# Delta stage of a two-layer hybrid encoder: the written order binds four engines instead of one

## The chip, the cores and the metric

The kernel runs on one core of one Trainium2 chip. The metric is the device time of one execution in microseconds. The core has five engines that run at the same time, each through its own list of instructions in order: TensorE (matrix products; PE in the profile, and PEld for its weight loads), VectorE (DVE), ScalarE (ACT), GpSimd (POOL) and SyncE (SP), which here only issues transfers. An instruction that needs another engine's result, or a buffer that is still in use, waits on a semaphore, and everything behind it in the same engine's list waits too.

## The reference

Input x is 1 x 2048 x 1024 in float32. Two layers follow one another, then a final RMSNorm. Each layer does this:

```
h = rms_norm(x); proj = h @ w_in                   # 1024 -> 5648 columns
# branch A: gated DeltaNet, 4 heads of 128, both directions
q, k, v = silu(depthwise_conv5(proj[...])); q, k L2-normalised
g = -exp(a_log) * softplus(a + dt_bias); beta = sigmoid(b)
# per chunk: (I + lmat) sol = [v*beta, k*beta*exp(g)]; scan over chunks with a 128x128 state per head
v_new = val - k_cum @ S;  o = q_dec @ S + attn @ v_new;  S = S * decay + k_dec^T @ v_new
o = rms_norm(o_forward + o_backward) * silu(z_a);  y_a = o @ w_dn_out
# branch B: GLU -> depthwise conv 31 -> LayerNorm -> silu, times silu(z_b);  y_b = (...) @ w_cf_out
gate = sigmoid(gate_lg + gate_b)                   # two gates of 1024 columns
x = x + (gate_a * y_a + gate_b * y_b) @ w_out
```

## The kernel before

**Layout.** Channels lie on the 128 partitions and tokens along the free dimension. A dense product takes each operand as a high part and a rest (`split`, lines 161 to 163) and sums three products, so a "dense step" (`dense_steps`, line 174) is three matmuls of 128x128 by 128x512 into one PSUM tile `pd`. Eight such steps make one block of 512 tokens by 128 output columns. A column's weights are loaded and split by `weight` (line 165), which has two buffers each for the high part, the rest and the raw load.

**Order of a layer.** The heads of branch A, the Conformer convolutions and the gate columns of the first half of the tokens come first; then `delta` (line 819), the stage that the change is about; then `merge` (line 1128).

**The Delta stage.** Chunks hold 128 tokens, so there are 16 steps (`NCH`). Step s handles chunk s in the forward direction and chunk 15 - s in the backward one. Its parts are Python generators:

- `fetch` loads a step's keys, queries and values for both directions (`kq`, `kv`) and has GpSimd scale the keys (line 855).
- `prep` makes the inverse of a step's triangular matrix for both directions and four heads. It loads Gram matrices (`dl<-gr`), decay rows (`dm<-gc`, rows spread to all partitions) and the 32x32 inverse blocks (`dh<-inv`); GpSimd adds a mask (line 885), ScalarE takes eight exponentials (line 888), VectorE makes four products of decay and Gram matrix (lines 889 and 890) and two transposes (line 883). Then four stages of small matmuls join 32x32 inverses to 64x64 and then to 128x128, with a ScalarE copy between the first and second (line 911) and between the third and fourth (line 935).
- `lane`, one per direction: in its first stage state times keys and state times queries; VectorE updates the values (line 970) and ScalarE scales the query result (line 961). In its second stage the inverse times the values, copied out by ScalarE (line 977). In its third stage the new state (VectorE, line 987) and the output; from step 8 on the other direction's output of that chunk is loaded back, GpSimd adds the query part (line 998) and VectorE the rest (line 999).
- `finish` normalises two finished chunks (ScalarE squares at line 1012, a reciprocal square root of small VectorE instructions at lines 195 to 201, ScalarE scalings at line 1023); `gate` transposes them on TensorE (line 89) and stores them.
- `pull(n)` takes n dense steps from a filler: the gate columns of the second half of the tokens (`gates(1)`, 256 steps), then an early part of the merge (`early_merge`, 64 steps). The counts are LEAD ahead of the loop, STEP inside a step and TAIL behind it. A filler that yields GAP ends the current step's pulls.

**What sets the order.** A planner orders each engine's instructions by the program's order as a priority and its own estimate of when each is ready, and sets the waits. `set_order` (line 98) chains TensorE's instructions of this stage in the order in which they are written; VectorE, ScalarE, GpSimd and the transfer queues are left to the planner. `prep` runs two steps ahead: steps 0 and 1 are prepared before the loop, and step s carries the four matmul stages of step s + 2. Buffers are rings cut out of larger tiles: four each for `kq` and `kv`, two for decay rows (one step's worth), four and six for Gram matrices, five for outputs, two for gate inputs.

Of the kernel before, what the change touches and what calls it, by code (L numbers as in the profile page):

```python
# [28 lines left out]
LEAD = (20, 8, 8, 6, 4)  # L29
STEP = (5, 4, 4, 3)  # L30
TAIL = (6, 8)
# [4 lines left out]
BIG = -1.0e30  # L36
NOSYNC = mybir.DependencyInfo(mybir.DependencyClass.NoSync, mybir.DependencyReason.DATA)
# [37 lines left out]
class Trunk:  # L75
    def __init__(self, tc, a, depth):
        self.tc, self.nc, self.a, self.depth = tc, tc.nc, a, depth
        self.back = deque()
        self.post = deque()
        self.credit = 0.0  # L80
        self.rate = 0.0
        self.inorder = False
        self.tail = None

    def matmul(self, *args, **kw):
        return self.queue(self.nc.tensor.matmul(*args, **kw))  # L86

    def transpose(self, *args):
        return self.queue(self.nc.tensor.transpose(*args))

    def queue(self, ins):
        if self.inorder:
            if self.tail is not None:
                self.tc.add_manual_dep(ins.ins, self.tail, NOSYNC, reason="TensorE order")
            self.tail = ins.ins.name
        return ins

    def set_order(self, on):
        self.inorder, self.tail = on, None
# [74 lines left out]
    def dense_steps(self, ps, w, xs, kk):  # L174
        mm = self.matmul
# [625 lines left out]
    def gates(self, half):  # L801
        nc = self.nc
        for j in range(16):
            w = self.weight(self.a["w_in"][self.l, 28 + j], KD)
# [14 lines left out]
    def delta(self):  # L819
# [26 lines left out]
        def fetch(step):  # L846
            out = []
            for d in range(2):
# [5 lines left out]
                k2 = col(self.kf, d, c)  # L854
                nc.gpsimd.tensor_tensor(out=kv[:, 0], in0=kv[:, 0], in1=k2[:, :, None].to_broadcast([P, 4, P]),
                                        op=ALU.mult)
                out.append((c, kq, kv))
            return out

        blk = lambda b: slice(32 * b, 32 * b + 32)  # L860
        lo, up = slice(0, 64), slice(64, 128)
        pairs = ((0, 1), (2, 3))

        def prep(step):
            ins, ks = [], []
# [3 lines left out]
            quads = range(4)  # L869
            for d in range(2):  # L870
                c = step if d == 0 else NCH - 1 - step
                g, k = hv(rgq()), hv(rgk())
                self.load(g, self.g_d[c][:, :, 1, :])
                self.load(k, self.g_d[c][:, :, 0, :])
                gb = hv(rgb())
                v32 = (dt if d == 0 else pt)[:, d]
                with nc.allow_non_contiguous_dma(reason="rows to all partitions and inverse blocks"):
                    r0 = d * 64 + c * 4
                    self.load(gb, self.gc_d[r0:r0 + 4][None].to_broadcast([P, 4, P]))
                    r4 = 64 * d + 4 * c  # L880
                    self.load(v32, self.inv_d[:, r4:r4 + 4, :].rearrange("h b (i j) -> (b i) h j", j=32))
                o32 = (pt if d == 0 else dt)[:, d]
                v_.transpose(o32.rearrange("p h c -> p (h c)"), v32.rearrange("p h c -> p (h c)"))
# [5 lines left out]
                v_.tensor_tensor(out=k, in0=k, in1=gb, op=ALU.mult)  # L889
                v_.tensor_tensor(out=g, in0=g, in1=gb, op=ALU.mult)  # L890
                ins.append(g)
                ks.append(k)
            yield
            wt = rwt().rearrange("p (m c) -> p m c", c=P)
# [7 lines left out]
            mm = self.matmul  # L902
# [46 lines left out]
        def lane(step, d, g, wt, c, kq, kv):  # L949
            mm = self.matmul  # L950
# [3 lines left out]

            def query():
                pq = hv(self.pz())
                for hd in range(H):
                    mm(pq[:, hd, :], kq[:, hd, 1, :], s[:, hd, :], start=True, stop=True)
                o1 = ro1()
                for hd in range(H):  # L960
                    nc.scalar.activation(hv(o1)[:, hd, :], pq[:, hd, :], AF.Copy, scale=eg[:, hd:hd + 1])  # L961
                return o1
# [345 lines left out]
```

## Time and profile before

| what | value |
|---|---|
| time, median of 3 runs | 3299.22 us (3292.3 to 3299.87) |
| the profiled execution's own time | 3296.47 us |
| its span, first to last instruction | 3294.7 us |
| TensorE / its weight loads / VectorE busy | 95% / 83% / 72% |
| ScalarE / GpSimd busy | 42% / 9% |
| mean granted TensorE clock | 0.981 |
| bytes moved by DMA | 501.69 MB, mean 152 GB/s |
| Delta stage, first product to last transpose | about 900 to 1329 us and 2507 to 2942 us |

Busy time of TensorE includes modelled ends of its pipelined matmuls. The granted clock is 1.00 at full rate; a stretch that shows less had a part at half rate. "Idle before" counts the time in which an engine had nothing running ahead of an instruction, with the one that ended the wait behind the arrow. Line 86 is a helper that records every matmul, so TensorE's work is told apart by tiles: `pd` is dense work, `pz` is the Delta stage's; `dl`, `dm` and `dh` are the tiles that the rings are cut from.

### The profile page before, as it was taken

The numbers are of one execution on the slowest core, as the hardware profiler recorded it, in microseconds if no ns is written. First come the engines' busy times: TensorE is split into PE (matmuls) and PEld (weight loads), VectorE is DVE, ScalarE is ACT, GpSimd is POOL, SyncE is SP. The second block draws the span as 40 slices with busy tenths as digits, with TensorE's granted clock in tenths as the row PEclk, the third lists the DMA queues.
The fourth block names the chain that finished last, engine by engine and source line by source line (L and its number), as shares of the span: only waits on it lengthen the run. The fifth ranks groups of instructions, "written<-read, shape, count | busy, mean of one in ns | idle before, by whom it ended". The sixth has DMA issues, their size and how long they took to land. (4 is left out here: it accounts for less than half of the span.)

```text
span 3294.7 us, 51078 instructions
## 1 busy us (share of the span) xinstructions
PE 3127.2 (95%) x19110; PEld 2727.5 (83%) x19110; DVE 2360.0 (72%) x4401; ACT 1391.8 (42%) x3104; POOL 303.4 (9%) x297
## 2 busy tenths in 40 slices
PE   6999999999999988999999999999999998998998
PEld 5888888888788878787888888888887887887786
DVE  7689989896555566745676989898864556567655
ACT  5625252523443456523344333343234444565332
POOL 3000000000121221000000000000002112200000
PEclk9999999999999999999999999999999999899999
DMA  4223131334676776654423232323457767756634
GB/s 140 89 94 109 65 109 65 110 115 161 225 248 219 245 219 196 193 184 129 140 62 94 76 101 87 97 80 97 154 194 235 238 220 216 231 180 199 202 124 150
DMA packets 425880, 501.69 MB, mean 152 GB/s; under 512 B 95584, under 2 KB 260064, under 8 KB 425632
## 3 DMA queue, kind: packets, MB, share of 16 engines
q1 hardware_dynamic: 352304, 387.53, 38.3%
q10 hardware_dynamic: 65264, 81.14, 7.1%
q0 software_dynamic: 8064, 29.76, 2.4%
q8 instruction: 150, 2.46, 0.3%
q14 instruction: 98, 0.80, 0.1%
HBM read 342.74 MB, written 155.58 MB: 151 GB/s over the span
## 5 line engine op out<-in xcount | busy, mean ns | idle before, releaser
L86 PE MATMUL pd<-hhi,whi 128*128 128x512 f32 x2816 | 1100.1, 391 | 0.0
L86 PE MATMUL pd<-hhi,wlo 128*128 128x512 f32 x2816 | 1078.2, 383 | 2.9 <-DVE wlo L163 2.9
L86 PE MATMUL pd<-hlo,whi 128*128 128x512 f32 x2816 | 1078.7, 383 | 0.0
L740 DVE SCALAR_TENSOR_TENSOR cacc<-gp,vec,cacc 128x1009 f32<-128x1009 f32 (+1 forms) x480 | 614.0, 1279 | 37.7 <-ACT cacc L738 34.6
L86 PEld LDWEIGHTS pd<-hhi,wlo 128*128 128x128 f32 x2816 | 538.2, 191 | 81.9 <-DVE wlo L163 4.5
L86 PEld LDWEIGHTS pd<-hhi,whi 128*128 128x128 f32 x2816 | 538.8, 191 | 81.0 <-issue 1.4
L86 PEld LDWEIGHTS pd<-hlo,whi 128*128 128x128 f32 x2816 | 539.1, 191 | 74.2 <-issue 1.9
L162 ACT ACTIVATE whi<-wraw 128x512 fp32r<-128x512 f32 x400 | 243.0, 624 | 437.1 <-PE pd L86 340.4
L163 DVE TENSOR_TENSOR wlo<-wraw,whi 128x512 fp32r<-128x512 f32 x400 | 272.7, 695 | 118.0 <-ACT whi L162 117.6
L565 DVE SCALAR_TENSOR_TENSOR acc<-cin,vec,acc 128x1022 f32<-128x1022 f32 (+1 forms) x192 | 246.4, 1298 | 15.0 <-ACT acc L563 13.9
L86 PE MATMUL pd<-yhi,wlo 128*128 128x512 f32 x512 | 195.3, 381 | 6.7 <-DVE wlo L163 6.5
L86 PE MATMUL pd<-yhi,whi 128*128 128x512 f32 x512 | 194.9, 381 | 2.1 <-ACT whi L162 2.0
L86 PE MATMUL pd<-ylo,whi 128*128 128x512 f32 x512 | 194.3, 379 | 1.7 <-DVE ylo L163 1.7
L888 ACT ACTIVATE dm<-dm,ngc 128x128 f32<-128x128 f32 x256 | 89.3, 403 | 216.8 <-POOL dm L885 214.7
L86 PEld LDWEIGHTS pz<-dh,dl 32*32 32x32 f32 (+2 forms) x2496 | 144.8, 148 | 26.7 <-DVE dl L889 10.0
L86 PE MATMUL pz<-dh,dl 32*32 32x32 f32 (+2 forms) x2496 | 151.6, 235 | 15.8 <-DVE dl L889 9.6
L86 PE MATMUL pd<-uop,whi 128*128 128x512 f32 x512 | 157.9, 390 | 6.5 <-ACT whi L162 6.5
L86 PE MATMUL pd<-gop,whi 128*128 128x512 f32 x512 | 153.8, 382 | 4.9 <-DVE gt L1164 3.4
L889 DVE TENSOR_TENSOR dl<-dl,dm 128x512 f32<-128x512 f32 x64 | 46.1, 721 | 153.7 <-ACT dm L888 113.1
L86 PEld LDWEIGHTS pz<-dm,dl 128*128 128x128 f32 x992 | 119.0, 198 | 17.0 <-issue 15.6
L86 PE MATMUL pz<-dm,dl 128*128 128x128 f32 x992 | 121.2, 282 | 10.0 <-ACT dm L977 9.7
L815 ACT ACTIVATE go<-pd,vec 128x512 f32<-128x512 f32 x128 | 87.7, 685 | 83.1 <-PE pd L86 73.0
(272 smaller groups left out, 4242.8 us busy)
## 6 DMA issues: line engine op xcount, KB each, us to landing
wraw<-w_in SPq DMA_DIRECT2D x240, 256.0 KB, 2.9
gt<-go ACTq DMA_DIRECT2D x128, 256.0 KB, 2.8
dl<-gr SPq DMA_DIRECT2D x128, 256.0 KB, 5.5
dl<-kq SPq DMA_DIRECT2D x64, 512.0 KB, 6.4
dl<-kv SPq DMA_DIRECT2D x64, 512.0 KB, 5.3
gt<-gt SPq DMA_DIRECT2D x64, 512.0 KB, 5.0
wraw<-w_out SPq DMA_DIRECT2D x96, 256.0 KB, 3.1
kq<-acc SPq DMA_DIRECT2D x16, 1024.0 KB, 5.4
```

The costliest lines, as they stand in the source:

```text
L86: return self.queue(self.nc.tensor.matmul(*args, **kw))
L162: self.nc.scalar.activation(hi, src, AF.Copy)
L163: self.nc.vector.tensor_tensor(out=lo, in0=src, in1=hi.bitcast(F32), op=ALU.subtract)
L565: self.nc.vector.scalar_tensor_tensor(out=out, in0=t[:, k:k + n], scalar=wc(k), in1=out, op0=ALU.mult, op1=ALU.add)
L740: self.nc.vector.scalar_tensor_tensor(out=acc, in0=t[:, k:k + n], scalar=wc(k), in1=acc, op0=ALU.mult, op1=ALU.add)
L815: nc.scalar.activation(cut(o), sort(ps), AF.Identity, bias=self.vec[:, V_GB + j:V_GB + j + 1])
L888: nc.scalar.activation(gb[:, hd, :], gb[:, hd, :], AF.Exp, bias=ng[:, hd:hd + 1])
L889: v_.tensor_tensor(out=k, in0=k, in1=gb, op=ALU.mult)
```

## The change

The manual chaining of TensorE's instructions goes. After the whole stage has been written, `bind` walks through its instructions and chains each to the one before it on the same engine, for TensorE, ScalarE, VectorE and GpSimd. Transfers on SP stay with the planner; those issued from ScalarE's queue are part of its order.

The text is then laid out as one pipeline. `prep` is cut into more stages: loads; mask and exponentials; transposes, copies and the four products; then the four matmul stages. The loads of step s + 3, the exponentials and products of step s + 2 and the matmul stages of step s + 1 stand in step s, so the inverse is one step ahead instead of two, and only step 0 is prepared whole before the loop. The scaling of the next step's keys is a function of its own (`decay_keys`). In `lane` the loading of the other direction's output and GpSimd's addition move from the third stage to the first. `finish` takes over `gate` and is cut into four stages that are spread over the following step. Weights in `gates` and `early_merge` are asked for one column ahead; the early merge's operands are loaded first and split one by one, with a GAP after each. LEAD, STEP and TAIL get other counts, and a GAP ends only the pull that meets it.

```
-LEAD = (20, 8, 8, 6, 4)
-STEP = (5, 4, 4, 3)
-TAIL = (6, 8)
+LEAD = (16, 6, 8, 6, 4)
+STEP = (5, 4, 4, 4)
+TAIL = (3, 3, 3)
+BOUND = (mybir.EngineType.PE, mybir.EngineType.Activation, mybir.EngineType.DVE, mybir.EngineType.Pool)
...
+    def bind(self, start):
+        last = {}
+        for ins in self.nc.cur_bb.bb.instructions[start:]:
+            if ins.engine in BOUND:
+                if ins.engine in last:
+                    self.tc.add_manual_dep(ins, last[ins.engine], NOSYNC, reason="written order")
+                last[ins.engine] = ins.name
...
     def gates(self, half):
+        ahead = self.weight(self.a["w_in"][self.l, 28], KD)
         for j in range(16):
-            w = self.weight(self.a["w_in"][self.l, 28 + j], KD)
+            w = ahead
+            if j < 15:
+                ahead = self.weight(self.a["w_in"][self.l, 29 + j], KD)
...
         def lane(step, d, g, wt, c, kq, kv):
+            o1 = old = None
+            if step >= NCH // 2:
+                old = ro()
+                self.load(old, od)
             if step:
...
+                if old is not None:
+                    nc.gpsimd.tensor_tensor(out=old, in0=old, in1=o1, op=ALU.add)
             yield
...
+        start = self.mark()
+        nil = iter(())
+        preps = [prep(i) for i in range(NCH)] + [nil, nil, nil]
+        go = lambda i: next(preps[i], None)
+        go(0)
         ins = fetch(0)
+        go(0)
+        go(0)
+        go(1)
         pull(LEAD[0])
+        go(1)
+        go(1)
+        for d in range(2):
+            decay_keys(ins[d], d)
+        for n in LEAD[1:4]:
+            go(0)
             pull(n)
+        go(2)
+        ready = go(0)
+        pull(LEAD[4])
+        last = finish([])
         for step in range(NCH):
             nxt = fetch(step + 1) if step + 1 < NCH else None
+            gs, wt = ready
             lanes = [lane(step, d, gs[d], wt, *ins[d]) for d in range(2)]
+            for x in lanes:
+                next(x)
+            go(step + 1)
+            if nxt:
+                for d in range(2):
+                    decay_keys(nxt[d], d)
+            go(step + 2)
+            next(last)
+            pull(STEP[0])
+            for x in lanes:
+                next(x)
+            next(last)
+            go(step + 2)
+            go(step + 1)
+            pull(STEP[1])
             for x in lanes:
                 next(x, None)
+            go(step + 1)
+            go(step + 3)
+            new = finish(list(done))
             done.clear()
+            next(new)
+            pull(STEP[2])
+            next(last)
+            ready = go(step + 1)
+            last = new
+            pull(STEP[3])
             ins = nxt
+        for n in TAIL:
             pull(n)
+            next(last)
         for _ in fill:
             pass
+        self.bind(start)
...
     def early_merge(self):
+        self.u0, load, split = self.operand_parts(self.u_d, 0, "uop")
         for k in range(4):
+            load(k)
         yield GAP
+        ahead = self.weight(self.a["w_cf"][self.l, 0], 4)
+        for k in range(4):
+            split(k)
+            yield GAP
```

## Prediction before the run

> **What bounds the kernel now.** I read the page first, then a table by stretches of the Delta stage, then who TensorE waits for in it, then the order of time on the engines inside one step.
>
> ```profile
> span 3294.7 us, 51078 instructions
> PE 3127.2 (95%) x19110; PEld 2727.5 (83%) x19110; DVE 2360.0 (72%) x4401; ACT 1391.8 (42%) x3104; POOL 303.4 (9%) x297
> ```
>
> TensorE is busy for 95% of the span, so what any reordering can win is the other 5% and what a slowed clock costs. The second view is the table of busy times by stretches (start:end, length, then busy us and count of PE, PEld, DVE, ACT, POOL, then the granted clock, DMA share, GB/s). Per layer the rows are: lead-in and step 0; step 1; steps 2 to 7; steps 8 to 12; steps 13 and 14; and, for the first layer only, what follows.
>
> ```profile
> 900.20:948.50 48.30, 42.69 (x511) 36.12 (x511) 23.64 (x53) 23.07 (x58) 12.28 (x10) 0.93 0.89 282
> 948.50:973.70 25.20, 22.39 (x242) 20.12 (x241) 14.13 (x39) 13.15 (x31) 4.62 (x4) 1.00 0.71 228
> 973.70:1118.60 144.90, 138.25 (x1441) 122.58 (x1440) 81.13 (x228) 57.14 (x168) 27.74 (x24) 0.98 0.70 225
> 1118.60:1256.50 137.90, 120.92 (x1234) 107.81 (x1234) 87.93 (x256) 71.70 (x247) 36.77 (x31) 0.96 0.73 227
> 1256.50:1300.60 44.10, 38.33 (x344) 35.06 (x343) 29.73 (x85) 28.26 (x84) 8.07 (x6) 0.88 0.68 221
> 1300.60:1329.10 28.50, 28.50 (x172) 25.94 (x171) 13.47 (x45) 18.53 (x55) 2.54 (x2) 1.00 0.54 151
> 2507.10:2559.00 51.90, 45.06 (x512) 38.06 (x512) 24.28 (x53) 22.77 (x58) 11.83 (x11) 0.90 0.85 273
> 2559.00:2583.20 24.20, 22.31 (x242) 20.09 (x241) 13.89 (x38) 13.15 (x31) 4.61 (x4) 1.00 0.69 217
> 2583.20:2726.80 143.60, 136.19 (x1442) 120.38 (x1441) 82.08 (x228) 57.14 (x168) 27.74 (x24) 1.00 0.71 227
> 2726.80:2869.60 142.80, 127.94 (x1234) 113.17 (x1233) 88.55 (x256) 71.80 (x247) 37.19 (x31) 0.90 0.71 218
> 2869.60:2913.40 43.80, 36.60 (x343) 33.81 (x342) 29.66 (x85) 28.06 (x83) 7.91 (x6) 0.92 0.67 219
> ```
>
> To know what of a step is waste I need its TensorE work at full clock. The pieces come from the timeline (start, us, engine, line, tiles, count, and the wait before it in brackets), the filler's price from the chain of waits (start, us, what).
>
> ```profile
> 2473.53 20.52 PE pd L86 x95
> ...
> 2618.05 0.62 PE L86 MATMUL pz<-dh,dh 32*32 32x32 f32 x48 [0.90 <-ACT dh L911]
> 2621.62 3.81 PE L86 MATMUL pz<-dm,dl 128*128 128x128 f32 x32 [0.17 <-ACT dm L977]
> ...
> 2777.35 1.04 PE L89 MATMUL pz<-con,dm 128*128 128x128 f32 x8
> 2778.32 0.68 PE L86 MATMUL pz<-dl,dh 64*64 64x64 f32 x16
> ...
> 2780.98 4.12 PE L86 MATMUL pz<-dh,dl 128*128 128x128 f32 x64
> 2788.04 1.05 DVE L199 TENSOR_TENSOR rst<-orr,rsv 128x8 f32<-128x8 f32 x1
> 2789.27 0.15 DVE L200 TENSOR_TENSOR rst<-rst,orr 128x8 f32<-128x8 f32 x1
> 2789.74 2.05 PE L86 MATMUL pz<-dl,dl 128*128 128x128 f32 x16 [1.21 <-DVE dl L970]
> 2791.00 2.45 ACT L1023 ACTIVATE dm<-dm,orr 128x128 f32<-128x128 f32 x8 [1.93 <-DVE orr L1020]
> ```
>
> State products with the inverse's first product 4.12, inverse's second 0.62, two products of 0.68 (one row stands for both), the triangular product 2.05, state and output products 3.81: 11.96 us. One filler step is three matmuls of 20.52/95 = 0.216, so 0.648; sixteen make 10.4. A step is worth 22.3 us, and 23.4 with the eight transposes (1.04) that appear from step 9.
>
> Length minus work, first layer and second. Lead-in with step 0 holds 42 fillers (27.2), three inverses of 2.4 (0.62 + 0.68 + 0.68, and 0.4 left of the 4.12 when thirty-two products go at the 3.81 row's rate), 2.05 and 3.81: 40.3, so 8.0 and 11.6 are lost. Step 1: 2.9 and 1.9. Steps 2 to 7 (133.8): 11.1 and 9.8. Steps 8 to 12 (115.9): 22.0 and 26.9. Steps 13 and 14 (two fillers, then sixteen without an inverse: 14.3 + 21.0): 8.8 and 8.5. What follows is full: nothing. In all 111.5 us; everything the change can win lies there. That includes the half-rate clock (11 us of it in steps 8 to 12 of layer one, by 2 x 0.04 x 137.9).
>
> Who ends the waits, second layer, first half and second half (us in total, times, longest):
>
> ```profile
> PE pz L86 <- ACT dh L911: 8.3, 7, 2.5
> PE pz L86 <- DVE dl L889: 4.4, 2, 3.6
> ...
> PE pz L86 <- ACT dh L911: 8.7, 5, 2.4
> PE pz L86 <- ACT dm L977: 3.9, 2, 2.5
> PE pz L86 <- DVE dl L970: 3.6, 3, 1.9
> ```
>
> L911 is the small ScalarE copy between the inverse's first two products. The timeline shows why it is late: eight scalings L1023 (2.45 us), themselves late behind a reciprocal square root on VectorE, stand ahead of it on ScalarE. That root's small steps are also mixed among the L970 updates for which the triangular product waited 1.21.
>
> **The change, part by part.** It removes no arithmetic. It fixes ScalarE's, VectorE's and GpSimd's order to the text's, so each wait now also holds whatever is written behind it. Prices, from the groups by line of steps 8 to 12, second layer (busy us, mean ns, idle before):
>
> ```profile
> L888 ACT ACTIVATE dm<-dm,ngc 128x128 f32<-128x128 f32 x40 | 13.9, 395 | 25.9 <-POOL dm L885 25.7
> L885 POOL TENSOR_TENSOR dm<-dm,con 128x512 f32<-128x512 f32 x10 | 13.2, 1318 | 21.1 <-DMA dm<-gc 18.7 <-ACT dm L961 2.4
> L998 POOL TENSOR_TENSOR dm<-dm,dm 128x512 f32<-128x512 f32 x10 | 12.7, 1274 | 20.2 <-ACT dm L961 19.5 <-DMA dm<-o 0.7
> L855 POOL TENSOR_TENSOR dl<-dl,kf 128x512 f32<-128x512 f32 x11 | 11.4, 1040 | 65.2 <-DMA dl<-kv 47.3 <-PE pd L86 9.0 <-PE pz L86 8.9
> L977 ACT ACTIVATE dm<-pz 128x512 f32<-128x512 f32 x10 | 5.5, 591 | 0.3
> L815 ACT ACTIVATE go<-pd,vec 128x512 f32<-128x512 f32 x10 | 6.8, 683 | 0.6 <-DMA dl<-gr 0.5
> L889 DVE TENSOR_TENSOR dl<-dl,dm 128x512 f32<-128x512 f32 x10 | 6.9, 689 | 23.2 <-ACT dm L888 19.5 <-POOL dm L998 3.7
> ```
>
> First-half step, from the start of the state products: these and the first inverse product end at 4.1, five fillers at 7.4, the triangular product at 9.4, the second inverse product at 10.1, four fillers at 12.7; then the next product needs L977's copy. ScalarE's written order ahead of that copy is: scaled queries (to about 5), L911, eight exponentials (3.2). These wait for two GpSimd masks behind two decays, 2 x 1.32 + 2 x 1.04 = 4.7 us. The loads are asked for a step earlier, in the same SP queue, so the masks end near 5 and the copy at about 10.7, against 12.7: covered, with 2 us over. L911 is now written ahead of every scaling and its use four fillers later. I keep 0.4 a step for what I have missed (between 0 and today's 1.7): steps 2 to 7 win 20.9 - 4.8 = 16, step 1 wins 4.8 - 1.0 = 3.8.
>
> Second-half step: the two L998 additions now stand ahead of the decays on GpSimd, because they are written into the lane's first stage. They need the scaled queries (about 3 and 5) and the loads of the old output. The chain is then 6.3 after two additions, 8.4 after the decays, 11.0 after the masks, 12.6 after the last exponentials, 13.2 after the copy, or 13.9 when one L815 falls between: 0.5 to 1.2 later than the 12.7 at which TensorE wants it. VectorE's products (four of 0.69) wait for the same exponentials, and behind them stand the inverse's copies and the state update: another 0.8 by the same addition. With 0.7 for the clock, 2.5 a step. Bounds: 0, and today's 4.9. Ten steps win 48.9 - 25 = 24.
>
> The clock, by the row: steps 8 to 12 of layer two show 0.90 though no wait listed there is longer than 2.5 us, and I charge for it. The Trainium skill, "TensorE: Matmul & The Clock Gate", section "What's actually happening", says that half rate follows an idle window of about 3.4 us. This trace disagrees, since shorter waits sufficed. By the rule my 0.7 a step would go, and the sum would be 7 us better.
>
> Lead-in: it prepares one inverse ahead of the loop instead of two, with 40 fillers instead of 46. ScalarE's written order puts the second inverse's exponentials ahead of the first's L911. Their row load shares buffers with the first's products: loads 5.2 (median below), four products 2.8, another load 5.2, mask 2.6, the last four exponentials 1.6, copy 0.3: 17.7, against a cover of 16 + 6 fillers and one product (14.7). So 3.0 remain, and about 2 for the clock: 5 a layer, between 0 and today's 8.0 and 11.6. Gain 19.6 - 10 = 9.6.
>
> Filler change-over: LEAD 46 and 16 a step leave 2 of the 256 gate fillers for step 13 today. LEAD 40 and 17 a step run out in step 12 after 12; the next five pulls each meet a gap (the operand loads, then four splits one by one), so steps 12 and 13 have 5 and 13 fewer where today one step has 14 fewer. The splits also stand in ScalarE's and VectorE's order now. I charge 10 a layer against 8.8 and 8.5: minus 3, between plus 6 and minus 12.
>
> Parts at nothing: weights asked for one column earlier and the load order (no wait of TensorE above names them); the tail (its row is full, PE 28.50 of 28.50, and 17 filler steps instead of 18 follow); step 0's stores moving to SP. Without that cover the tail's ScalarE and VectorE work would cost about 5 us a layer, from 2.45 and its neighbours.
>
> Sum: 16 + 3.8 + 24 + 9.6 - 3 = 50. The profiled execution's 3296.5 less 50 is 3246; the median of the runs (3299.2) stands 2.7 above that execution, so I forecast 3249 us.
>
> **The rivals.** (1) *Slower: the old output arrives late.* Place: steps 8 to 13, GpSimd's first addition. Issues on SP and the landing times of these tiles:
>
> ```profile
> 2781.69 0.60 SPq L150 DMA_DIRECT2D dm<-o  x1
> ...
> 2815.01 0.42 SPq L150 DMA_DIRECT2D dm<-o  x1
> DMA to landing us min/median/max: 2.8/5.2/7.9
> ```
>
> The steps begin at 2780.98 and 2809.53, so these went out 0.7 and 5.5 in; with 5.2 they land 6 to 11 in, where 5 is wanted. Today only an addition late in the step waits; in the written order decays, masks, exponentials and the state's copy all stand behind it. Each us costs TensorE one: 12 for twelve steps. Landing 4 us later than I allow eats the gain; 11 to 13 in gives 3249 + 12 x 7 = 3333. Against it: the load is written ahead of the state products, earlier than now.
>
> (2) *VectorE blocked by GpSimd.* One root step took 1.05 us (L199) while a mask ran, its neighbour 0.15. In the written order all fourteen follow the L970 updates, just when GpSimd works without a pause; VectorE then reaches the products 2 us later, and steps 8 to 12 keep today's 4.9: 3249 + 24 = 3273, up to 3285 if the first half keeps half of its own. The Trainium skill, "SBUF — State Buffer", section "Who interferes with whom", has this as a rule: a VectorE instruction with two SBUF inputs is blocked whole by a GpSimd one that reads SBUF; the L199 row agrees.
>
> (3) *Nearly all waits go.* If loads land early and the splits hide, only the change-over and the lead-in keep about 20: 3299 - 91 = 3208. The idle 58% of ScalarE speaks for it.
>
> (4) *No change:* the planner's order was as good on average, and each wait removed reappears elsewhere: 3299.
>
> **How the numbers follow.** Forecast (3235 to 3270) 0.42, rival 2 0.13, rival 3 0.17, no change 0.10, slower 0.18. About 0.3%, 10 us, is what a measurement of this kernel can tell from none. Faster 0.42 + 0.13 + 0.17 = 0.72; same 0.10; slower 0.18. The range runs from just below rival 3 to just past no change, 3203 to 3312, leaving out most of rival 1.
>
> **What would show it.** Right: steps 2 to 7 near 23 us each (17 fillers), TensorE's waits on L911 and L970 gone, in steps 8 to 12 a wait of 1 to 2 us on the copy of the triangular product, and 4 to 8 us lost in step 13. Wrong: GpSimd idle for the old output ahead of its additions (rival 1), VectorE's root steps near 1 us and waits on the state update (rival 2), or new waits on L911 in the lead-in beyond 5 us.

## The result, and the profile after

The changed kernel takes 3320.5 us (median of 4 runs, 3318.6 to 3326.9) against 3299.6 us for the kernel before (median of 4 in the same comparison). The ratio is 1.0069, with a 95% interval of 1.0047 to 1.0092: 21 us slower. The forecast was 3249 us with a range that ended at 3312. The sign was wrong, and the time lies outside of the range.

The head of the page of the changed kernel:

```profile
span 3316.8 us, 50988 instructions
...
PE 3129.0 (94%) x19110; PEld 2725.5 (82%) x19110; DVE 2397.4 (72%) x4401; ACT 1400.9 (42%) x3104; POOL 299.4 (9%) x297
```

The arithmetic is the same on every engine, and the span is 22 us longer. The table by stretches (columns as in the prediction) tells where. The rows are steps 13 and 14 of the first layer, then of the second layer the lead-in with step 0, steps 1 to 7, 8 to 12, 13 and 14, and the stretch from step 15 to the first product of the merge's output gate.

```profile
1250.57:1316.40 65.83, 47.66 (x468) 42.86 (x465) 38.88 (x102) 34.90 (x109) 11.50 (x10) 0.82 0.53 169
2510.58:2571.31 60.73, 50.89 (x445) 42.82 (x444) 26.83 (x54) 22.84 (x51) 13.89 (x12) 0.92 0.87 278
2571.31:2739.70 168.39, 163.31 (x1702) 146.01 (x1701) 98.88 (x266) 73.45 (x200) 31.09 (x27) 0.99 0.73 232
2739.70:2870.82 131.12, 120.35 (x1234) 106.87 (x1232) 97.43 (x250) 71.86 (x242) 34.97 (x30) 0.97 0.73 227
2870.82:2935.36 64.54, 45.55 (x466) 40.84 (x464) 37.91 (x102) 34.00 (x107) 11.52 (x10) 0.84 0.53 169
2935.36:2974.87 39.51, 38.52 (x211) 33.39 (x209) 21.34 (x57) 25.20 (x65) 2.56 (x2) 1.00 0.58 172
```

Steps 13 and 14 stand out: 64.5 us with TensorE busy for 45.6, at a granted clock of 0.84. To compare kernels whose steps hold different numbers of fillers, I take from each stretch's length the work of its own matmuls at full clock, as the prediction did, but counted one by one: 0.216 us for a filler matmul, 0.117 for a 128x128 one (3.81 us for 32, less the modelled end of the last), 0.042, 0.013 and 0.13 for the two small shapes and a transpose. For the changed kernel that makes 47.3, 159.3, 114.7, 39.2 and 37.4 us a layer. The row of steps 13 and 14 above then loses 64.54 - 39.2 = 25.3. Counted like this the kernel before loses 116.6 us in both layers (the prediction, by pieces of a step, had 111.5).

| kernel (loss in us, both layers) | time, us | ratio to before, 95% | lead-in, step 0 | 1-7 | 8-12 | 13-14 | rest | sum |
|---|---|---|---|---|---|---|---|---|
| before | 3299.6 | 1 | 20.3 | 28.3 | 51.2 | 18.2 | -1.4 | 116.6 |
| forecast | 3249 | | 10 | 5.8 | 25 | 20 | 0 | 61 |
| changed kernel | 3320.5 | 1.0047 to 1.0092 | 27.2 | 18.6 | 33.5 | 52.1 | 3.3 | 134.7 |
| e1_uop | 3302.6 | 0.9992 to 1.0018 | 26.8 | 22.1 | 32.0 | 33.4 | 3.7 | 118.0 |
| e2_weights | 3283.4 | 0.9936 to 0.9965 | 21.2 | 8.8 | 21.1 | 50.3 | -0.4 | 101.0 |
| e3_both | 3260.6 | 0.9850 to 0.9911 | 19.7 | 9.0 | 17.5 | 34.9 | -0.4 | 80.7 |
| e4_pe_only | 3254.4 | 0.9832 to 0.9899 | 12.7 | 31.5 | 5.2 | 15.0 | -0.2 | 64.2 |
| e5_no_gpsimd | 3227.6 | 0.9764 to 0.9804 | 20.2 | 5.3 | -0.4 | 24.4 | -0.1 | 49.4 |
| e6_first_half | 3244.4 | 0.9800 to 0.9852 | 15.1 | 13.2 | 15.6 | 18.2 | -0.4 | 61.7 |
| e7_add_late | 3234.2 | 0.9784 to 0.9824 | 21.1 | 7.0 | -0.4 | 24.5 | -0.4 | 51.8 |
| e8_old_text | 3525.3 | 1.0665 to 1.0710 | 58.2 | 81.1 | 91.9 | 58.3 | 54.7 | 344.2 |
| e9_add_only | 3273.2 | 0.9894 to 0.9932 | 27.4 | 23.4 | 1.9 | 38.2 | 3.1 | 94.0 |
| e10_lead | 3217.5 | 0.9732 to 0.9768 | 2.6 | 15.7 | -0.4 | 22.3 | -0.4 | 39.8 |
| e11_step16 | 3225.4 | 0.9750 to 0.9784 | 20.8 | 1.6 | -0.2 | 16.5 | -0.8 | 37.9 |
| e12_all | 3205.0 | 0.9691 to 0.9728 | 2.7 | 3.9 | -0.2 | 16.1 | -0.9 | 21.6 |

The sums carry the times: time less sum lies between 3178 and 3190 in every row. That spread, some 12 us, comes from one execution to the next and from outside of the stage (its first load starts between 883.8 and 891.4 us in the builds, with nothing changed ahead of it), so the columns tell smaller differences apart than the times do.

Against the kernel before, steps 1 to 12 gained 27 us; the lead-in lost 7, steps 13 and 14 lost 34, and the rest lost 5. Who ends TensorE's waits in the changed kernel: the lead-in of the second layer, steps 8 to 12 of the second layer, steps 13 and 14 of the first; and whom GpSimd waits for, in two rows for steps 8 to 12 and in the last for steps 13 and 14 of the second layer (us in total, times, longest).

```profile
PE pd L175 <- DVE wlo L157: 7.9, 1, 7.9
...
PE pz L992 <- ACT dm L985: 5.0, 3, 2.9
PE pz L1001 <- DVE dh L931: 3.4, 3, 1.7
...
PE pz L992 <- ACT dm L985: 7.9, 1, 7.9
PE pz L983 <- ACT dm L977: 5.2, 1, 5.2
...
POOL dm L979 <- ACT dm L977: 77.9, 6, 20.1
POOL dm L979 <- DMA dm<-o: 22.6, 1, 22.6
...
POOL dm L979 <- DMA dm<-o: 3.3, 1, 3.3
```

Four things are to be read here. The longest wait in the lead-in names a *weight split* (L157, the rest of a split operand), which no line of the prediction had on its list. Line 985, the copy of the triangular product, waits for 8 us in step 13. Line 931 is one of the inverse's copies on VectorE. And GpSimd's addition of the old output (L979) waits in steps 8 to 12 six times for the scaled queries of its own step and once for the load of the old output; in step 13 that load ends a wait again.

**The lead-in.** The timeline of the second layer's (start, us, engine, line, tiles, count, wait before):

```profile
2511.60 2.63 DVE L902 COPY dl<-dh 32x256 f32<-32x256 f32 x4 [10.38 <-POOL dl L839]
...
2516.59 0.69 DVE L906 TENSOR_TENSOR dl<-dl,dm 128x512 f32<-128x512 f32 x1 [1.63 <-DMA dl<-gr]
2517.20 1.29 DVE L908 TENSOR_TENSOR dl<-dl,dm 128x512 f32<-128x512 f32 x2
2518.40 1.29 DVE L157 TENSOR_TENSOR wlo<-wraw,whi 128x512 fp32r<-128x512 f32 x2
...
2519.14 0.79 PE L175 MATMUL pd<-hhi,wlo 128*128 128x512 f32 x1 [7.94 <-DVE wlo L157]
```

VectorE's order has the first inverse's copies and products ahead of the filler's split, as they are written there. The copies wait for GpSimd to clear their buffer, a product waits for its Gram matrix, and the split stands behind both, with the fillers that were to cover just these waits.

**Step 9, second layer.** Same columns, engines mixed by time:

```profile
2768.18 1.05 PE L968 MATMUL pz<-dh,dl 128*128 128x128 f32 x8
2770.32 1.12 ACT L977 ACTIVATE dm<-pz,eg 128x128 f32<-128x128 f32 x4
2771.52 1.27 POOL L979 TENSOR_TENSOR dm<-dm,dm 128x512 f32<-128x512 f32 x1 [19.25 <-ACT dm L977]
2773.17 1.28 POOL L979 TENSOR_TENSOR dm<-dm,dm 128x512 f32<-128x512 f32 x1 [0.39 <-ACT dm L977]
2773.32 1.15 DVE L1032 TENSOR_TENSOR oss<-oss,cq 128x8 f32<-128x8 f32 x1
2774.41 2.04 POOL L857 TENSOR_TENSOR dl<-dl,kf 128x512 f32<-128x512 f32 x2
2776.41 2.50 POOL L889 TENSOR_TENSOR dm<-dm,con 128x512 f32<-128x512 f32 x2
2777.71 2.50 ACT L892 ACTIVATE dm<-dm,ngc 128x128 f32<-128x128 f32 x8 [4.45 <-POOL dm L889]
2777.74 1.20 DVE L194 TENSOR_TENSOR rst<-rst,orr 128x8 f32<-128x8 f32 x1
2780.12 1.05 ACT L985 ACTIVATE dm<-pz 128x512 f32<-128x512 f32 x2
2780.84 1.13 PE L992 MATMUL pz<-dm,dl 128*128 128x128 f32 x8
2785.03 0.29 DVE L931 COPY dh<-pz 32x128 f32<-32x128 f32 x1
2785.46 1.13 PE L1001 MATMUL pz<-dm,dl 128*128 128x128 f32 x8 [1.70 <-DVE dh L931]
```

GpSimd stood idle for 19 us ahead of L979 with decays (L857) and masks (L889) behind it, since the scaled queries that the addition needs don't exist before this step's own products. Only then did the masks run, and the exponentials (L892) and the copy (L985) after them.

**Step 13, first layer**, the same view:

```profile
1249.24 4.52 SPq L144 DMA_DIRECT2D uop<-u  x4
1255.96 2.48 SPq L144 DMA_DIRECT2D dm<-o  x1
1257.18 1.06 ACT L156 ACTIVATE uop<-uop 128x1024 fp32r<-128x1024 f32 x1 [3.26 <-DMA uop<-u]
1258.14 2.16 ACT L977 ACTIVATE dm<-pz,eg 128x128 f32<-128x128 f32 x8
1259.35 1.28 POOL L979 TENSOR_TENSOR dm<-dm,dm 128x512 f32<-128x512 f32 x1 [20.92 <-ACT dm L977]
1263.79 1.26 POOL L979 TENSOR_TENSOR dm<-dm,dm 128x512 f32<-128x512 f32 x1 [3.16 <-PE pz L983]
1268.30 2.50 ACT L892 ACTIVATE dm<-dm,ngc 128x128 f32<-128x128 f32 x8 [7.82 <-POOL dm L889]
1270.70 1.04 ACT L156 ACTIVATE uop<-uop 128x1024 fp32r<-128x1024 f32 x1
1271.64 1.05 ACT L985 ACTIVATE dm<-pz 128x512 f32<-128x512 f32 x2
1272.36 2.04 PE L992 MATMUL pz<-dm,dl 128*128 128x128 f32 x8 [7.94 <-ACT dm L985]
```

ScalarE's order has a split of the merge's operand (L156) ahead of the query scaling. It waits for its load; the scaling comes at 1258.14, 7.6 us into the step; the first addition waits for the scaling, which ends at 1260.30. The second starts at 1263.79, 3.2 us after the first has ended. The row puts that wait down to a product (L983), but in the second layer the same wait, 3.3 us, is put down to the load of the old output, and that load goes out late here too: its issue stands at 1255.96, 5.4 us into the step, behind the operand's four loads in SP's list. The masks wait for the additions, the exponentials for the masks and the copy for the exponentials, with a second operand split between. This step has hardly a filler to cover it.

### The profile page after: what moved, and what is told of

It is laid out like the page before. It is cut to its first block, busy times and chain, and to the rows that moved or that the text cites. A ratio compares the mean times of both kernels' runs of the same rounds, so it can differ in the third digit from the quotient of the medians.

```text
span 3316.8 us, 50988 instructions
## 1 busy us (share of the span) xinstructions
PE 3129.0 (94%) x19110; PEld 2725.5 (82%) x19110; DVE 2397.4 (72%) x4401; ACT 1400.9 (42%) x3104; POOL 299.4 (9%) x297
## 5 line engine op out<-in xcount | busy, mean ns | idle before, releaser
L175 PE MATMUL pd<-hhi,wlo 128*128 128x512 f32 x2816 | 1075.1, 382 | 18.6 <-DVE wlo L157 18.6
L156 ACT ACTIVATE whi<-wraw 128x512 fp32r<-128x512 f32 x400 | 242.5, 623 | 483.2 <-PE pd L174 312.2
L157 DVE TENSOR_TENSOR wlo<-wraw,whi 128x512 fp32r<-128x512 f32 x400 | 276.4, 706 | 217.4 <-ACT whi L156 216.7
L535 ACT ACTIVATE cin<-pd 128x512 f32<-128x512 f32 x96 | 57.0, 594 | 156.8 <-PE pd L175 156.6
L1192 ACT ACTIVATE gt<-gt 128x1024 f32<-128x1024 f32 x64 | 67.6, 1057 | 114.9 <-DMA gt<-gt 100.8
L175 PEld LDWEIGHTS pd<-yhi,wlo 128*128 128x128 f32 x512 | 96.7, 189 | 22.0 <-DVE wlo L157 8.5
L973 DVE SCALAR_TENSOR_TENSOR dl<-pz,neg,dl 128x128 f32<-128x128 f32 x240 | 66.8, 345 | 66.2 <-PE pz L968 65.9
L892 ACT ACTIVATE dm<-dm,ngc 128x128 f32<-128x128 f32 x256 | 80.2, 391 | 81.1 <-POOL dm L889 80.8
L173 PEld LDWEIGHTS pd<-yhi,whi 128*128 128x128 f32 x512 | 96.8, 189 | 20.3 <-ACT whi L156 7.1
L173 PE MATMUL pd<-uop,whi 128*128 128x512 f32 x256 | 100.2, 391 | 11.9 <-ACT uop L156 6.4
L746 ACT ACTIVATE ao<-pd 128x512 f32<-128x512 f32 x64 | 38.3, 598 | 170.0 <-PE pd L175 169.9
```

The lines of the kernel that those rows point to most:

```text
L156: self.nc.scalar.activation(hi, src, AF.Copy)
L157: self.nc.vector.tensor_tensor(out=lo, in0=src, in1=hi.bitcast(F32), op=ALU.subtract)
L173: mm(ps, whi[:, k, :], xhi, start=k == 0, stop=False)
L175: mm(ps, wlo[:, k, :], xhi, start=False, stop=k == kk - 1)
L535: nc.scalar.activation(cut(t[:, o + b * NB:o + (b + 1) * NB]), sort(ps), AF.Copy)
L892: nc.scalar.activation(gb[:, hd, :], gb[:, hd, :], AF.Exp, bias=ng[:, hd:hd + 1])
```

## The experiments

The first theory from these rows: filler work in the order of other engines costs time, the operand splits in step 13 and the weight splits in the lead-in. Two edits tell the two apart, with this addition to `split` (the weights' splits in one, the operand's in the other):

```
+        if loose: self.loose |= {a.ins.name, b.ins.name}
...
-            if ins.engine in BOUND:
+            if ins.engine in BOUND and ins.name not in self.loose:
```

**e1_uop**: the operand's splits are left to the planner.

> The changed kernel with one thing taken out of the written order: the four splits of the early merge's operands (ScalarE and VectorE, eight instructions a layer) are left to the planner. Theory 1, the splits' place in the order: in step 13 ScalarE's scaling of the query result stands behind the first split, which waits for its operand to land, and the state's copy behind the second. Steps 13 and 14 lose 28.6 and 27.3 us now (length less work); that falls by about 12 a layer, so about 3296 us. Rival, late transfers: the other direction's output still lands some 13 us into step 13, because its load stands behind the operand loads in SP's queue; GpSimd's chain stays and the gain is under 5 us a layer, so 3310 or more.

Measured 3302.6 us, 18 less than the changed kernel. It comes from where it should: steps 13 and 14 fall from 52.1 to 33.4, the other columns stay within 4. The time lies between the two expectations, and the rival holds in part: in step 13 GpSimd still waits 3.9 us in the first layer and 3.6 in the second for the load of the old output, and TensorE's wait on the copy is 9.5 and 9.1 us.

**e2_weights**: the weights' splits are left to the planner.

> The changed kernel with the splits of the fillers' weights left to the planner, everything else bound. Theory 1: the wait of 8.2 and 7.9 us that TensorE has in the lead-in on VectorE's part of a weight split goes, because that split no longer stands behind the inverse's products, which wait for their Gram matrices. With the half-rate clock behind it about 9 us a layer, so about 3302 us. Rival: the lead-in is set by its transfers (their engines are nearly full there), the same wait turns up at the inverse's first product, and the gain is under 3 us a layer, so 3314 or more.

Measured 3283.4 us, 37 less, twice what the lead-in's wait alone could give. The lead-in gives 6; steps 1 to 7 give 10 and steps 8 to 12 another 12. The weight splits cost in steps 1 to 12 too, not in the lead-in alone: the waits of TensorE on the inverse's copy L931 in steps 1 to 7, 4.4 us in the first layer and 3.3 in the second, are no longer listed.

**e3_both**: both kinds are left to the planner.

> Both kinds of split left to the planner. Theory 1: the two gains add, about 42 us, so about 3278 us, faster than the kernel before. Rival, late transfers: 3300 to 3312 us.

Measured 3260.6 us, 60 less and 17 below the expectation: 18 and 37 add, and 5 us are over. With that the change is faster than the kernel before by 1.2%.

**e4_pe_only**: the new text, with TensorE alone bound as in the kernel before.

```
-BOUND = (mybir.EngineType.PE, mybir.EngineType.Activation, mybir.EngineType.DVE, mybir.EngineType.Pool)
+BOUND = (mybir.EngineType.PE,)
```

> The changed kernel's text with TensorE alone bound, as in the kernel before. If the binding of the three other engines is what costs, the time falls to the kernel before's or below, 3280 to 3300 us. If the new text costs (fillers used up earlier, five gaps instead of one, one inverse ahead), it stays at 3312 us or more, with the same 13 fewer fillers in step 13.

Measured 3254.4 us, 26 below the range for the case that the binding costs. So the new text by itself wins 45 us, and binding the three other engines takes 66 away. The columns show both sides of binding: against this kernel, e3_both wins 22 in steps 1 to 7 and loses 12 in steps 8 to 12, 20 in steps 13 and 14 and 7 in the lead-in. Something else than the splits is badly placed from step 8 on. What begins there is the old output.

**e5_no_gpsimd**: as e3_both, and GpSimd is left to the planner.

```
-BOUND = (mybir.EngineType.PE, mybir.EngineType.Activation, mybir.EngineType.DVE, mybir.EngineType.Pool)
+BOUND = (mybir.EngineType.PE, mybir.EngineType.Activation, mybir.EngineType.DVE)
```

> Edit: as the version in which the splits of both operands are left to the planner (3260.6 us), and GpSimd's instructions too; ScalarE, VectorE and TensorE stay in the written order. Theory (what binding still costs there, about 10 us a layer in steps 13 and 14 and 5 in steps 8 to 12 against TensorE alone bound, comes from GpSimd's chain: additions of the old output written ahead of decays and masks): GpSimd can then run a mask ahead of an addition whose load is late, and steps 8 to 14 get back 10 to 15 us a layer, 3230 to 3245. Rival (the cost is ScalarE's and VectorE's own order: copies and squares standing ahead of the copy that TensorE wants): GpSimd's freedom changes nothing, 3255 to 3265, with the wait on the copy of the triangular product in step 13 still near 11 us.

Measured 3227.6 us, a little better than the theory's range. Steps 8 to 12 lose nothing any more (-0.4), steps 13 and 14 lose 24 instead of 35. In steps 8 to 12 GpSimd's order was the rest of the cost; ScalarE's and VectorE's own orders were not. In steps 13 and 14 this version still loses 9 us more than the one with TensorE alone bound (24.4 against 15.0), and which of the two orders costs them no run here tells.

**e7_add_late**: as e3_both, all four bound, with one line of the text moved: GpSimd's addition goes back to the lane's third stage, where the kernel before had it.

```
                 for hd in range(H):
                     nc.scalar.activation(hv(o1)[:, hd, :], pq[:, hd, :], AF.Copy, scale=eg[:, hd:hd + 1])
-                if old is not None:
-                    nc.gpsimd.tensor_tensor(out=old, in0=old, in1=o1, op=ALU.add)
...
             if old is not None:
+                nc.gpsimd.tensor_tensor(out=old, in0=old, in1=o1, op=ALU.add)
                 v_.tensor_tensor(out=old, in0=po, in1=old, op=ALU.add)
```

> Edit: the splits left to the planner, all four engines bound, and GpSimd's addition of the old output moved back from the lane's first stage to its third, behind the triangular product, where the text before had it. Theory (the addition that waits for the old output's load delays decays, masks, exponentials and the state's copy behind it): steps 8 to 12 and 13 to 14 lose less, 3240 to 3252, and the wait on the copy in step 13 falls from 11 us to under 5. Rival (the copy is late for another reason, such as the squares and output products on ScalarE and VectorE): 3257 to 3270, the later addition only delaying the outputs.

Measured 3234.2 us, 6 below the theory's range and far from the rival's. Steps 8 to 12 again lose nothing, and steps 13 and 14 lose 24.5, as with GpSimd free. TensorE's wait on the copy in step 13 falls from 11.1 and 11.3 us (e3_both, by layer) to 2.7 and 2.6. So it is this one instruction's place, and not that GpSimd is bound.

**e6_first_half**: as e3_both, with ScalarE, VectorE and GpSimd bound in steps 0 to 7 only.

```
+        for n, ins in enumerate(self.nc.cur_bb.bb.instructions[start:], start):
+            if ins.engine != mybir.EngineType.PE and not a <= n < b:
+                continue
```

> Edit: the splits left to the planner, and ScalarE, VectorE and GpSimd held to the written order only in steps 0 to 7; in the lead-in and from step 8 on TensorE alone is held. Theory (binding helps where nothing late stands in the order, that is in steps 1 to 7, and costs where the old output and the change-over come in): lost time a layer about 7 in the lead-in, 4.5 in steps 1 to 7, 3 in steps 8 to 12, 7.5 in steps 13 and 14, together 22 against 40 (both sorts of splits loose) and 32 (TensorE alone held): 3225 to 3240. Rival (the gain of steps 1 to 7 is only moved: what is not waited for there is waited for later, since the gate fillers run out at the same place): no better than TensorE alone held, 3250 to 3260.

Measured 3244.4 us, between the two ranges. The lead-in came out as in the theory (15.1), steps 1 to 7 and 13 and 14 lost 3 to 4 us more; but steps 8 to 12 lost 15.6 where TensorE alone bound loses 5.2. TensorE's longest wait there, 2.5 us in the first layer and 4.0 in the second, is on the small copy between the inverse's first two products (L923 in this kernel). Why the planner orders these steps worse behind a bound first half I did not find out.

**e8_old_text**: the text before, with its four engines bound.

```
     def set_order(self, on):
-        self.inorder, self.tail = on, None
+        if on:
+            self.tail = len(self.nc.cur_bb.bb.instructions)
+            return
+        last = {}
+        for ins in self.nc.cur_bb.bb.instructions[self.tail:]:
+            if ins.engine in BOUND:
+                if ins.engine in last:
+                    self.tc.add_manual_dep(ins, last[ins.engine], NOSYNC, reason="written order")
+                last[ins.engine] = ins.name
```

> Edit: the text before, with ScalarE, VectorE and GpSimd held to its written order as well as TensorE. It tells what the rewriting of the text is worth under the same binding. Theory (an order written without regard to loads is ruinous when held, since masks, products and splits are written right behind the loads they need): every step waits for a load of about 5 us and the masks behind it, 6 to 10 us a step over 30 steps in the two layers: 3480 to 3600. Rival (the rewriting matters little, the splits' waits are the main cost of holding an order whatever the text): about 60 us slower than the kernel before, 3350 to 3370.

Measured 3525.3 us, ratio 1.0665 to 1.0710. The time is the theory's, but TensorE's waits are mostly the rival's kind: the list of who ends them (same columns as above) is led by ScalarE's weight split, with VectorE's products far behind.

```profile
PE pd L87 <- ACT whi L167: 171.0, 59, 17.5
PE pz L87 <- DVE dl L894: 42.1, 22, 3.9
```

Holding an order that wasn't written for it is the worst of all, 205 us worse than the changed kernel.

**e9_add_only**: the changed kernel with e7's line moved and nothing else; the splits stay bound.

> Edit: the changed kernel with one thing moved: GpSimd's addition of the old output goes back from the lane's first stage to its third; the splits stay in the written order and all four engines are bound. Theory (the splits and the addition are two separate costs that add, as the two kinds of splits did): the addition is worth what it was worth with the splits loose, about 26 us, so 3320 less 26, 3288 to 3300. Rival (the wait on the operand splits in step 13 covers the addition's lateness, so that with the splits bound little is won): 3308 to 3320.

Measured 3273.2 us, 47 less than the changed kernel and 0.7 to 1.1% *faster* than the kernel before. Both ranges missed it. The addition and the splits don't add: alone they cost 47 and 60, together 86 (3320.5 - 3234.2), so some 21 us are had by mending either (12 by the sums of the columns, where they cost 41, 54 and together 83). The columns place the overlap in steps 8 to 12: 33.5 falls to 1.9 by the addition, to 17.5 by the splits, and to -0.4 by both. The same step 9 in this kernel:

```profile
2748.39 1.05 PE L968 MATMUL pz<-dh,dl 128*128 128x128 f32 x8
2749.31 2.95 POOL L889 TENSOR_TENSOR dm<-dm,con 128x512 f32<-128x512 f32 x2
2750.13 2.68 DVE L157 TENSOR_TENSOR wlo<-wraw,whi 128x512 fp32r<-128x512 f32 x2 [3.46 <-ACT whi L156]
2752.23 2.97 POOL L1001 TENSOR_TENSOR dm<-dm,dm 128x512 f32<-128x512 f32 x2
2753.39 2.45 ACT L892 ACTIVATE dm<-dm,ngc 128x128 f32<-128x128 f32 x8
2755.94 0.17 DVE L194 TENSOR_TENSOR rst<-rst,orr 128x8 f32<-128x8 f32 x1
2756.87 0.60 ACT L983 ACTIVATE dm<-pz 128x512 f32<-128x512 f32 x1 [1.02 <-PE pz L981]
```

The masks end 3.9 us into the step instead of 10.7 and the exponentials 7.5 instead of 12.0; the copy (now L983) then waits for TensorE, not TensorE for the copy. The root's step L194 on VectorE takes 0.17 us where it took 1.20.

Two costs were left in e5_no_gpsimd: 10 us a layer in the lead-in and 12 in steps 13 and 14. Its lead-in, second layer:

```profile
2474.70 0.45 PE L918 MATMUL pz<-dh,dl 32*32 32x32 f32 x32
...
2482.08 1.26 POOL L892 TENSOR_TENSOR dm<-dm,con 128x512 f32<-128x512 f32 x1 [1.29 <-DMA dm<-gc]
...
2485.83 0.28 ACT L921 ACTIVATE dh<-pz 128x128 f32<-128x128 f32 x1
...
2486.16 0.28 PE L928 MATMUL pz<-dh,dh 32*32 32x32 f32 x4 [6.93 <-ACT dh L921]
```

The small copy (L921) of a product that ended at 2475.2 runs at 2485.8, behind the second inverse's exponentials, whose mask waited for a row load: the wait that the prediction had named.

**e10_lead**: e5_no_gpsimd with the first inverse's stages written ahead of the second's exponentials and products.

```
         pull(LEAD[0])
-        go(1)
-        go(1)
         for d in range(2):
             decay_keys(ins[d], d)
-        for n in LEAD[1:4]:
-            go(0)
-            pull(n)
+        go(0)
+        go(1)
+        pull(LEAD[1])
+        go(0)
+        go(1)
+        pull(LEAD[2])
+        go(0)
+        pull(LEAD[3])
```

> Edit: on the version with splits and GpSimd left to the planner (3227.6 us), the text of the lead-in is reordered: the first inverse's small copy is written ahead of the second inverse's exponentials, and the second inverse's copies and products behind the first's second stage. Theory (the 7 us wait of TensorE on that copy in each layer's lead-in comes from the exponentials written ahead of it): the wait goes, the lead-in loses 3 to 5 us instead of 10, 3212 to 3220. Rival (the exponentials and products are merely late somewhere else, at the second inverse in step 0): a new wait of about 5 us in step 0 or 1, 3223 to 3232.

Measured 3217.5 us, the theory's time, by both mechanisms: the lead-in loses 2.6 instead of 20.2, and 10.4 of that come back in steps 1 to 7, as the rival said. Waits on the same copy, 4.1 and 5.3 us, now stand in step 1.

**e11_step16**: e5_no_gpsimd with 16 fillers a step.

```
-STEP = (5, 4, 4, 4)
+STEP = (5, 4, 4, 3)
```

> Edit: on the same version, 16 fillers a step instead of 17, so that gate fillers are left for step 13 (40 + 13 x 16 = 248 of 256). Theory (steps 13 and 14 lose 11 to 14 us a layer because step 13 has almost no filler): with 8 of them there the loss falls to 6 to 8 a layer, and steps 1 to 12, which lose almost nothing now, have room for one less: 3215 to 3222. Rival (the seventeenth filler is what keeps steps 1 to 12 full): each of 24 steps loses 0.6 or more, 3228 to 3240.

Measured 3225.4 us, which can't be told from e5's 3227.6. The stage itself gained 11.5 us (steps 13 and 14 fall from 24.4 to 16.5, steps 1 to 7 from 5.3 to 1.6); what hides it lies outside of the stage, in the spread named above: the profiled execution takes 5.4 us more than e5's ahead of the first layer's stage and 3.3 more between the two stages, where nothing was changed. The seventeenth filler was not needed in the full steps.

**e12_all**: both edits together.

> Edit: the two edits before together, the reordered lead-in and 16 fillers a step, with splits and GpSimd left to the planner. Theory (both work and add): 3200 to 3210. Rival (one of them fails): the time of the better one, 3213 to 3225.

Measured 3205.0 us, ratio 0.9691 to 0.9728: the fastest version, 96 us under the kernel before in the same comparison and 115 under the changed kernel. The stage gains more than the two edits' sum (27.8 against 9.6 and 11.5), since the waits that e10_lead had moved into step 1 are gone (3.9 in steps 1 to 7); why one filler less does that I did not follow up. Of the second layer, the row of steps 8 to 12:

```profile
2656.28:2770.94 114.66, 114.66 (x1233) 104.21 (x1232) 91.51 (x253) 74.27 (x251) 37.60 (x31) 1.00 0.87 269
```

TensorE is busy in all of steps 8 to 12. Of the 22 us that the stage still loses, 16 lie in steps 13 and 14.

## Why the prediction was wrong

The forecast sum was a gain of 50; the stage lost 18. By the table the stage keeps 134.7 us where the forecast left 61. Of the 74 between, 32 lie in the change-over, 17 in the lead-in, 13 in steps 1 to 7, 9 in steps 8 to 12 and 3 behind step 15. Step by step:

**Lead-in (predicted a gain of 9.6, measured a loss of 6.9).** Two misses. The edit "weights asked for one column earlier" was put at nothing because no wait of TensorE in the Delta stage of the profile before named a weight split. Outside of the stage the same view did name them: VectorE's part (L163) ended 16 waits, 14.8 us in all, and ScalarE's (L162) ten, 8.5 us. And the reason holds only while the planner may move a split past a late product; the written order fixed it behind the products, and it cost a wait of 8 us in each layer. Letting the weights' splits loose took 6 us off this stretch. And the wait that was priced, the exponentials ahead of the first small copy, was the right mechanism at half its size: 3.0 us expected, 7.0 and 6.9 measured in the two layers once the wait before it was gone (e5_no_gpsimd); e10_lead, which takes the exponentials out of the way, brought the stretch from 20.2 to 2.6. In the changed kernel the wait for the split came first and hid most of it.

**Steps 1 to 7 (predicted a gain of 20, measured 9.7).** The mechanism was right: the waits on the small copy are nearly gone (0.4 and 0.8 us are left in the changed kernel), and with the splits and GpSimd free these steps lose 5.3 us, against 5.8 forecast. What was left out is again the fillers' splits in the order: letting the weights' splits loose brings the changed kernel's 18.6 to 8.8. Bound and unbound can be compared directly: 31.5 with TensorE alone held, 5.3 with ScalarE and VectorE held too and the splits left free.

**Steps 8 to 12 (predicted a gain of 24, measured 17.7).** The chain was priced well: additions done 6.3 us into the step, decays 8.4, masks 11.0, exponentials 12.6 by the prediction; 6.3, 8.3, 10.7 and 12.0 in step 9. Not priced in full was what it does to VectorE. I charged 0.8 for it; of the small steps at and ahead of the root, five ran beside GpSimd's work in step 9 and took 0.96 to 1.20 us, where e9_add_only has 0.17 to 0.29, 4.4 us more in all. The products behind them also need the exponentials, which ended at 2780.21, so not all of that was lost: by my estimate from these rows the inverse's copies came 2 to 3 us late, and TensorE's output product waited 1.70 for one of them (L931). This is rival 2's price, inside the likeliest case. (The row on which rival 2 was built, L199's 1.05 us, ran beside an addition, L998 from 2787.79 to 2789.06, and not beside a mask.) By the Trainium skill, "SBUF — State Buffer", "Who interferes with whom", a VectorE instruction with two inputs in SBUF contends with a GpSimd instruction that reads SBUF. The 1.20 of L194 beside a mask and its 0.17 in e9_add_only, with GpSimd idle, agree; two of the five, L1033 and L189, read only one tensor and were slowed all the same, to 0.97 and 0.96. The larger fault is another: I took the chain of additions, decays and masks as the price of these steps and did not ask what the same steps cost with the additions behind the masks. They cost 1.9. The prediction's 11 us for the clock in these steps of the first layer is also too much: 2 x 0.04 x 137.9 is the time at half rate, and at most half of it is lost.

**Change-over (predicted a loss of 3, measured 34).** This is the largest error, 31 us, and a term that was mis-sized. The steps were named (gaps, four splits one by one, fewer fillers, splits in ScalarE's order), and I charged 10 a layer from what the kernel before loses there. What the runs show in its place, in both layers: the operand's splits 19 (52.1 to 33.4), the addition 14 (52.1 to 38.2), the one and the other together 28 (52.1 to 24.5, e7_add_late, where the weights' splits are loose too), and of the rest the missing fillers 8 (24.4 to 16.5). The charge added small waits; in the trace they stand in one row, each behind the one before, from the loads of the operand and of the old output to TensorE, without a filler to cover them. The clock adds to it: by the granted 0.82 and 0.84, up to 0.18 x 65.8 + 0.16 x 64.5 = 22 us of the 52 are lost to it, and less as far as TensorE was idle in that time.

**Parts at nothing.** The stretch behind step 15 lost 4.7 us in both layers, half of the 5 a layer given for the case that its cover went; with the weights' splits loose it is full again. Step 0's stores show in no wait.

**The rivals.** Rival 1 (the old output late, 3333 us) came closest and had the right place, GpSimd's first addition, with decays, masks, exponentials and copy behind it. Its cause was wrong in most steps: in the second layer's steps 8 to 12 the load ended one of the listed waits, the scaled queries six. In step 13 it was right for the second addition, which waited 3.2 and 3.3 us for the load. And it was given 0.18 because the load is asked for earlier, which doesn't help where the load isn't what is waited for. Moving that line alone makes the change 0.9% faster than the kernel before. Rival 3's time, 3208 us, was reached by e12_all (3205.0), but with the splits and GpSimd left to the planner and the lead-in written anew.

What stays open: the 12 to 21 us that the splits and the addition share can be given to neither; why steps 8 to 12 of e6_first_half lose 15.6; which order costs the 9 us in steps 13 and 14 of e5_no_gpsimd; and which part of the new text wins the 45 us of e4_pe_only, since it was not taken apart.

## What to carry to other kernels

When an order is held on an in-order engine, each instruction inherits the waits of everything written ahead of it, so price not only the waits that the profile shows, but every instruction that the planner could have moved past one: above all a filler's own helper work on the other engines, which has to stay free to cover. Write a consumer as late as its use allows, not as early as its load: one addition on an engine that was 9% busy, written ahead of work that it didn't feed, cost 47 us, and 26 with the splits left free. Test a new text and a new binding apart, and bind engine by engine.

## What was not expected of the hardware

The contention between GpSimd and VectorE lengthens instructions on both sides. In step 9 of e9_add_only two weight splits on VectorE took 2.68 us, and the two masks that ran beside them 2.95; in the changed kernel's step 9, where masks ran beside small steps only, two masks took 2.50, and two splits with GpSimd idle 1.29 (the lead-in's row). The prediction had looked at VectorE's side alone.
